# Attention scores of one layer as 64-row float32 products, and feed-forward transposes in groups of eight

## The chip, the cores and the metric

The kernel runs on one core of one Trainium2 chip. The metric is device time in microseconds of one execution. TensorE (PE) multiplies, VectorE (DVE) and ScalarE (ACT) do element-wise work and empty the accumulators, GpSimd (POOL) does small vectors, and SyncE (SP) issues all DMA transfers.

## The reference

Two decoder layers over 256 tokens of width 1024, all in float32. What matters here of a layer:

```
q, k, v, s_in, c_in, g_in = split(rms_norm(x) @ w_in)
qh, kh = partial_rope(q), partial_rope(k)        # 8 query heads, 2 key heads, head width 64
scores = qh . kh * 64 ** -0.5                    # each token sees the 128 tokens up to itself
m = max(max(scores), sink);  pr = exp(scores - m)
y_attn = (pr / (sum(pr) + exp(sink - m)) @ v) @ w_attn_out
y_ssm, y_conv = (state-space branch of s_in), (convolution branch of c_in)
x = x + (gates[0] * y_attn + gates[1] * y_ssm + gates[2] * y_conv) @ w_mix_out
f_gate, f_up = split(rms_norm(x) @ w_ffn_in)     # hidden width 2816
x = x + (silu(f_gate) * f_up) @ w_ffn_out
x = x + sigmoid(rms_norm(x) @ w_ple_gate) * (p @ w_ple_in)
```

## The kernel before

The tokens are two tiles of 128 (`t` = 0, 1) and lie on the partitions. Every large product is a `gemm` (lines 447 to 479): pairs of 128-row blocks of a weight matrix are loaded as float32 (`raw`), ScalarE rounds them to float32r (`wh`), VectorE takes the difference (`wl`), and for each token tile and block TensorE adds three products of 512 columns, high by high, high by low and low by high. Left operands are brought to the same two parts by `split` (lines 229 to 234): a ScalarE copy and a VectorE difference. Transposes (line 281) are TensorE products with a float32 identity; they go to two banks of PSUM named `tr`, accumulators to four banks named `mm`, the attention's and the state-space branch's products to two named `sm`.

The order of the work is made while the program is built. A `gemm` calls `pump` (lines 391 to 400) after each six products. The small work is written as generators (`Stream`), each with a priority; they stop at points such as `on_pe`, `on_dve`, `on_act`, and `pump` runs a stream on if the planner's clocks (`run`, lines 122 to 142, with a cost per instruction) say that what it needs is ready. Each engine then works through its own list in that fixed order. In layer 0 the order of the gemms is `zk zq zc g00 g10 g11 g21 g01 y0 g20 y1 u1 c0 c1 u0 u2 u3` (line 34): the projections, the gates `g`, the attention output `y` (tiles `ya`), the state-space output `u`, the convolution output `c` (tiles `yc`).

Attention (`attn_stream`, lines 834 to 926) runs once for each token tile. The keys are transposed (`kTp`), and for each of the two key heads `split` writes a 128-row copy `kz` in which the rows of the other head are zeroed by the factor `pick[g]`. The queries are transposed four times, two heads in 128 rows each (`qTp`, `qT`). Scores go to two banks; each starts with a product of the identity and the mask, and then

```
for x, y in ((0, 0), (0, 1), (1, 0)):
    mm(o, qT[x][:, c, :], kz[y][:, :, 0:nk], False, x == 1 and i == n // 2 - 1)
```

adds three float32r products that give two heads at once. Tile 0 has 128 keys and one round of eight heads; tile 1 has 256 keys and two rounds of four. VectorE takes the row maxima (line 877), ScalarE the exponentials (line 885), TensorE transposes them (`pT`) and multiplies them with the values in float32 (`po`, line 913). Beside it run the state-space branch (`ssm_prep`: `P`, `prep`, `PTi`, `CAr`, `CAi`, `kt`; `ssm_stream`: `Xr`, `Xi`, `yx`, `ge`, `gy`, `gtm`, `sT`) and the convolution (`conv_stream`: `cacc`, `cT`, `cn`, `yl`, `yt`, `cTh`).

The feed-forward input has eleven gemms `fz` of 48 products for each layer. `e_fz` (lines 1282 to 1302) empties one: a tanh for each token tile, two VectorE passes (`fth`), four transposes into one bank (`hT`), and a `split` into `hdh` and `hdl`. The feed-forward output `fo` reads these pairs in order, `hid[k // 2]`, from the first on (line 1312).

Of the kernel before, what the change touches and what calls it, by code (L numbers as in the profile page):

```python
# [6 lines left out]
F32 = mybir.dt.float32  # L7
F32R = mybir.dt.float32r
# [8 lines left out]
NT = 2  # L17
# [64 lines left out]
def trunk_kernel(tc, wts, par, bmat, cst_d, x_d, pos_d, pt_d, bias_d, fg_d, out_d, dbg=None):  # L82
# [3 lines left out]
    with ctx:  # L86
# [8 lines left out]
        def b2(shape, dt=F32, name="b2"):  # L95
            return act.tile(shape, dt, tag="b2", bufs=25, name=name)
# [56 lines left out]
        def p_tr(name):  # L153
            return rotate(ps.tile([128, 512], F32, tag="tr", bufs=2, name=name), "tr", 2)
# [74 lines left out]
        def split(hi, lo, src, scale=None):  # L229
            copy(hi, src, scale)  # L230
            if scale is None:
                tt(lo, src, hi.bitcast(F32), ALU.subtract)
            else:
                stt(lo, src, scale, hi.bitcast(F32), ALU.mult, ALU.subtract)
# [44 lines left out]
        def transpose(out, in_):  # L279
            run("pe", PE_TR, [out], [in_])  # L280
            PE.transpose(out, in_, ident)
# [120 lines left out]
        def on_pe(*tiles, into=None):  # L402
            if into is None:
                n = f"tr.{(turn.get('tr', -1) + 1) % 2}"
                banks = [(n, 0), (n, 1)] if TRCHK else []
            else:
                banks = [k for b in into for k in keys(b)]
            return "pe", tiles, banks
# [423 lines left out]
            tt(z2, ra[:, 2], ra[:, 3], ALU.add)  # L832

        def attn_stream(t, S):
            zqk, vt, kz, par_l = S["zqk"], S["vt"], S["kz"], S["par"]
            nk = 128 * (t + 1)
            hpt = 1024 // nk
            mk = maskr[:, 256 - nk:256]
            z = zqk[t]
            yield lambda: S["rope_ok"]  # L840
            yield on_dve(z)
            rope_step(t, z)
            yield on_pe(z)
            zf = z.rearrange("p h d -> p (h d)")
            pt = p_tr("kTp")
            transpose(pt[:, 0:128], zf[:, 512:640])
            for g in range(2):
                split(kz[0][:, g, 128 * t:128 * t + 128], kz[1][:, g, 128 * t:128 * t + 128], pt[:, 0:128], pick[g])
            S["k_done"] += 1
            pt = p_tr("qTp")  # L850
            for k in range(4):
                transpose(pt[:, k * 128:k * 128 + 128], zf[:, k * 128:k * 128 + 128])
            qT = [b2([128, 4, 128], F32R, name=f"qT{i}") for i in range(2)]
            split(*[w.rearrange("p a b -> p (a b)") for w in qT], pt, 0.125)
            yield lambda: S["k_done"] > t
            st = act.tile([128, 6, 8], F32, tag="ast", bufs=4, name="ast")
            sink = par_l[:, O_SINK:O_SINK + 8]
            scs = []
            for b in range(8 // hpt):
                sc = b4([128, hpt, nk], name="sc")  # L860
                scs.append(sc)
                yield from sm_units.take(2)
                pts = [p_sm("sc").rearrange("p (i k) -> p i k", k=nk) for _ in range(2)]
                yield on_pe(*qT, *kz, into=pts)
                n = hpt // 2
                for hf in range(2):
                    mm(pts[hf], identr, bc(mk, 1, n), True, False)
                    for i in range(n // 2):
                        c = (hpt * b + n * hf) // 2 + i
                        o = pts[hf][:, 2 * i:2 * i + 2]  # L870
                        for x, y in ((0, 0), (0, 1), (1, 0)):
                            mm(o, qT[x][:, c, :], kz[y][:, :, 0:nk], False, x == 1 and i == n // 2 - 1)
                sl = slice(hpt * b, hpt * b + hpt)
                for hf in range(2):
                    yield on_dve(pts[hf])
                    run("dve", 615, [st], [pts[hf]])
                    DVE.reduce_max(out=st[:, 0, hpt * b + n * hf:hpt * b + n * hf + n], in_=pts[hf], axis=AX.X)
                yield on_dve(st)
                tt(st[:, 1, sl], st[:, 0, sl], sink[:, sl], ALU.max)
                tt(st[:, 2, sl], sink[:, sl], st[:, 1, sl], ALU.subtract)  # L880
                ts(st[:, 1, sl], st[:, 1, sl], -1.0, ALU.mult)
                for i in range(hpt):
                    yield on_act(st)
                    slot = hpt * b + i
                    func(sc[:, i], pts[i // n][:, i % n], AF.Exp, bias=st[:, 1, slot:slot + 1],
                         accum_out=st[:, 4, slot:slot + 1])
                sm_units.give(2)
            yield on_act(st)
            func(st[:, 3, :], st[:, 2, :], AF.Exp)
            yield on_dve(st)  # L890
            tt(st[:, 4, :], st[:, 4, :], st[:, 3, :], ALU.add)
            recip(st[:, 5, :], st[:, 4, :])
            pTs = {}
            for g in range(2):
                for kb in range(t + 1):
                    yield on_pe(*scs)
                    pt = p_tr("pT")
                    for i in range(4):
                        slot = 4 * g + i
                        transpose(pt[:, i * 128:i * 128 + 128],  # L900
                                  scs[slot // hpt][:, slot % hpt, kb * 128:kb * 128 + 128])
                    pT = b2([128, 4, 128], name="pTs")
                    copy(pT.rearrange("p h q -> p (h q)"), pt)
                    pTs[g, kb] = pT
            yield from sm_units.take(1)
            po = p_sm("po")
            yield on_pe(*pTs.values(), into=[po])
            for g in range(2):
                for i in range(4):
                    slot = 4 * g + i  # L910
                    kv = slot % 2
                    for kb in range(t + 1):
                        mm(po[:, slot * 64:slot * 64 + 64], pTs[g, kb][:, i, :], vt[kb][:, kv * 64:kv * 64 + 64],
                           kb == 0, kb == t)
            o = b2([128, 8, 64], name="o")
            yield on_dve(po, st)
            tt(o, po.rearrange("p (h d) -> p h d", h=8), bc(st[:, 5, :], 2, 64), ALU.mult)
            sm_units.give(1)
            yield on_pe(o)
            of = o.rearrange("p h d -> p (h d)")  # L920
            pt = p_tr("oT")
            for k in range(4):
                transpose(pt[:, k * 128:k * 128 + 128], of[:, k * 128:k * 128 + 128])
            hi, lo = b2([128, 4, 128], F32R, name="aTh"), b2([128, 4, 128], F32R, name="aTl")
            split(hi.rearrange("p a b -> p (a b)"), lo.rearrange("p a b -> p (a b)"), pt)
            S["aT"][t] = (hi, lo)
# [164 lines left out]
        def layer(l, feat, sts, prep):  # L1091
# [4 lines left out]
            hrstd = [stat(sts, 5, t) for t in range(NT)]  # L1096
            S["zqk"] = [act.tile([128, 10, 64], F32, tag="zqk", bufs=2, name="zqk") for t in range(NT)]
            S["vt"] = [act.tile([128, 128], F32, tag="vt", bufs=2, name="vt") for t in range(NT)]
            S["kz"] = [b2([128, 2, 256], F32R, name="kz") for i in range(2)]
            S["Ux"] = Ux = b2([128, 8, 64], name="Ux")  # L1100

            def e_zk(acc):
# [179 lines left out]
            def e_fz(acc):  # L1282
                yield on_act(*acc)
                ths = []
                for t in range(NT):
                    th = b1([128, 256], name="fth")
                    func(th, acc[t][:, 0:256], AF.Tanh, scale=stat(fst, 5, t))
                    ths.append(th)
                for t in range(NT):
                    yield on_dve(ths[t])  # L1290
                    stt(ths[t], ths[t], 1.0, acc[t][:, 0:256], ALU.add, ALU.mult)
                for t in range(NT):
                    stt(ths[t], acc[t][:, 256:512], stat(fst, 6, t), ths[t], ALU.mult, ALU.mult)
                yield on_pe(*ths)
                pt = p_tr("hT")
                for t in range(NT):
                    for k in range(2):
                        o = (2 * t + k) * 128
                        transpose(pt[:, o:o + 128], ths[t][:, k * 128:k * 128 + 128])
                hi, lo = b2([128, NT, 2, 128], F32R, name="hdh"), b2([128, NT, 2, 128], F32R, name="hdl")  # L1300
                split(hi.rearrange("p t k q -> p (t k q)"), lo.rearrange("p t k q -> p (t k q)"), pt)
                hid.append((hi, lo))

            for c in range(11):
                gemm(fT[0], 8, "fz", FFNB, e_fz, fT[0].need if c == 0 else None)
            split(pTh.rearrange("p a b -> p (a b)"), pTl.rearrange("p a b -> p (a b)"),
# [345 lines left out]
```

## Time and profile before

| | |
|---|---|
| median of 3 runs | 827.81 us (827.27 to 830.09) |
| profiled execution, its own time | 828.6 us |
| its span, first to last instruction | 826.8 us |
| mean granted clock of TensorE | 0.996 of full |
| TensorE busy | 810.5 us, 98% |
| VectorE, ScalarE busy | 575.9 us (70%), 479.8 us (58%) |

[...] A float32 product that is not a transpose has two records. In the timeline and the chain a line gathers equal instructions that follow each other.

### The profile page before, as it was taken

The numbers are of one execution on the slowest core, as the hardware profiler recorded it, in microseconds if no ns is written. First come the engines' busy times: TensorE is split into PE (matmuls) and PEld (weight loads), VectorE is DVE, ScalarE is ACT, GpSimd is POOL, SyncE is SP. The second block draws the span as 40 slices with busy tenths as digits, with TensorE's granted clock in tenths as the row PEclk, the third lists the DMA queues.
The fourth block names the chain that finished last, engine by engine and source line by source line (L and its number), as shares of the span: only waits on it lengthen the run. The fifth ranks groups of instructions, "written<-read, shape, count | busy, mean of one in ns | idle before, by whom it ended". The sixth has DMA issues, their size and how long they took to land.

```text
span 826.8 us, 11001 instructions
## 1 busy us (share of the span) xinstructions
PE 810.5 (98%) x3904; PEld 672.6 (81%) x3904; DVE 575.9 (70%) x876; ACT 479.8 (58%) x783; POOL 115.7 (14%) x310
## 2 busy tenths in 40 slices
PE   8999999899999999999999999999999999999996
PEld 6787888778888888888888888878888888888885
DVE  4589998696676875554578789877766666655455
ACT  6678856665546665553664675667554445445363
POOL 6784000000837000000110000100010000000011
PEclk9999999999999999999999999999999999999999
DMA  7755536456656655666655453766666666666661
GB/s 260 235 174 148 148 113 185 133 166 203 188 174 186 179 174 164 184 179 204 178 153 161 158 158 106 232 206 202 178 194 193 185 182 179 191 188 180 202 186 68
DMA packets 43685, 146.33 MB, mean 177 GB/s; under 512 B 4976, under 2 KB 6384, under 8 KB 43632
## 3 DMA queue, kind: packets, MB, share of 16 engines
q1 hardware_dynamic: 43632, 145.65, 58.3%
q8 instruction: 30, 0.49, 0.2%
q14 instruction: 23, 0.19, 0.1%
HBM read 144.58 MB, written 1.05 MB: 176 GB/s over the span
## 4 chain that ended last, share of the span: by engine, by line
PE 85%; DVE 5%; ACT 4%; DMA 3%; issue 1%; SPq 0%; POOLq 0%; POOL 0%; ACTq 0%; DVEq 0%
PE fz L227 27%; PE g L227 15%; PE fo L227 14%; PE mo L227 5%; DMA raw<-in_wts 3%; PE ya L227 2%; PE pz L227 2%; DVE wl L200 2%; PE u L227 2%; PE zc L227 2%; ACT wh L176 2%; PE pl L227 1%; PE zq L227 1%; PE ez L227 1%; PE yx L227 1%; PE po L227 1%
## 5 line engine op out<-in xcount | busy, mean ns | idle before, releaser
L200 DVE TENSOR_TENSOR wl<-raw,wh 128x1024 fp32r<-128x1024 f32 (+1 forms) x261 | 315.9, 1213 | 196.9 <-ACT wh L176 196.8
L176 ACT CAST wh<-raw 128x1024 fp32r<-128x1024 f32 (+1 forms) x261 | 272.4, 1046 | 187.9 <-PE fo L227 57.1
L200 POOL TENSOR_TENSOR nst<-nst 128x2 f32<-128x2 f32 (+1 forms) x14 | 2.8, 200 | 494.2 <-ACT sqj L171 493.7
L227 PE MATMUL fz<-wh,f0h 128*128 128x512 f32 x176 | 70.1, 398 | 0.0
L227 PE MATMUL fz<-wh,f1h 128*128 128x512 f32 x176 | 69.6, 395 | 0.0
L227 PE MATMUL fo<-wh,hdh 128*128 128x512 f32 x176 | 68.8, 391 | 0.0
L227 PE MATMUL fz<-wh,f0l 128*128 128x512 f32 x176 | 68.7, 390 | 0.0
L227 PE MATMUL fz<-wh,f1l 128*128 128x512 f32 x176 | 68.6, 390 | 0.0
L227 PE MATMUL fz<-wl,f0h 128*128 128x512 f32 x176 | 68.6, 390 | 0.0
L227 PE MATMUL fz<-wl,f1h 128*128 128x512 f32 x176 | 68.6, 390 | 0.0
L227 PE MATMUL fo<-wh,hdl 128*128 128x512 f32 x176 | 68.5, 389 | 0.0
L227 PE MATMUL fo<-wl,hdh 128*128 128x512 f32 x176 | 68.5, 389 | 0.0
L227 PEld LDWEIGHTS fz<-wh,f0l 128*128 128x128 f32 x176 | 33.0, 188 | 7.1
L227 PEld LDWEIGHTS fz<-wh,f1l 128*128 128x128 f32 x176 | 33.0, 188 | 7.0
L227 PE MATMUL g<-wh,h1h 128*128 128x512 f32 x96 | 38.2, 398 | 0.6 <-ACT g L171 0.6
L227 PEld LDWEIGHTS fo<-wh,hdl 128*128 128x128 f32 x176 | 33.0, 188 | 6.9
L227 PEld LDWEIGHTS fo<-wl,hdh 128*128 128x128 f32 x176 | 33.0, 188 | 6.8
L227 PEld LDWEIGHTS fo<-wh,hdh 128*128 128x128 f32 x176 | 33.0, 188 | 6.7
L227 PE MATMUL g<-wh,h0h 128*128 128x512 f32 x96 | 38.5, 401 | 0.0
L227 PEld LDWEIGHTS fz<-wl,f1h 128*128 128x128 f32 x176 | 33.1, 188 | 6.5
L227 PEld LDWEIGHTS fz<-wh,f1h 128*128 128x128 f32 x176 | 33.1, 188 | 6.5
L227 PEld LDWEIGHTS fz<-wl,f0h 128*128 128x128 f32 x176 | 33.1, 188 | 6.4
(377 smaller groups left out, 1739.5 us busy)
## 6 DMA issues: line engine op xcount, KB each, us to landing
raw<-in_wts SPq DMA_DIRECT2D x258, 512.0 KB, 3.6
brow<-in_bias SPq DMA_DIRECT2D x20, 256.0 KB, 4.3
raw<-in_wts SPq DMA_DIRECT2D x4, 256.0 KB, 3.8
out<-e SPq DMA_DIRECT2D x4, 256.0 KB, 2.0
x<-in_x SPq DMA_DIRECT2D x4, 128.0 KB, 3.8
x<-in_x SPq DMA_DIRECT2D x2, 256.0 KB, 5.4
bm<-in_bmat SPq DMA_DIRECT2D x4, 128.0 KB, 6.0
pT<-in_pt SPq DMA_DIRECT2D x2, 256.0 KB, 4.4
```

Of the source, the lines that this page charges most:

```text
L176: ACT.copy(out=out, in_=in_)
L200: (eng or DVE).tensor_tensor(out=out, in0=a, in1=b, op=op)
L227: PE.matmul(out, lhsT, rhs, start=start, stop=stop, skip_group_check=onto)
```

## The change

In layer 0 the keys are kept once, in float32 (`kT`, one ScalarE copy for each tile), and so are the queries (`qT`, one scaled copy). For each head one float32 product is made from the 64 rows in which the head lies: rows 0 to 63 for the heads of the first bank, 64 to 127 for those of the second. The two banks then hold every other head, and the maxima and exponentials are addressed accordingly. Layer 1 keeps the zero-padded keys. In the feed-forward of both layers `e_fz` keeps the result of every other gemm back, and transposes two together into both banks `tr`; the eleventh is alone.

```diff
@@ attn_stream
             pt = p_tr("kTp")
             transpose(pt[:, 0:128], zf[:, 512:640])
-            for g in range(2):
+            if kT is not None:
+                copy(kT[:, 128 * t:128 * t + 128], pt[:, 0:128])
+            for g in range(2 if kT is None else 0):
                 split(kz[0][:, g, 128 * t:128 * t + 128], kz[1][:, g, 128 * t:128 * t + 128], pt[:, 0:128], pick[g])
...
-            qT = [b2([128, 4, 128], F32R, name=f"qT{i}") for i in range(2)]
-            split(*[w.rearrange("p a b -> p (a b)") for w in qT], pt, 0.125)
+            if kT is None:
+                qT = [b2([128, 4, 128], F32R, name=f"qT{i}") for i in range(2)]
+                split(*[w.rearrange("p a b -> p (a b)") for w in qT], pt, 0.125)
+            else:
+                qT = [b2([128, 4, 128], name="qT")]
+                copy(qT[0].rearrange("p a b -> p (a b)"), pt, 0.125)
...
-                yield on_pe(*qT, *kz, into=pts)
+                yield on_pe(*qT, *(kz if kT is None else [kT]), into=pts)
                 n = hpt // 2
                 for hf in range(2):
                     mm(pts[hf], identr, bc(mk, 1, n), True, False)
-                    for i in range(n // 2):
+                    rows = slice(64 * hf, 64 * hf + 64)
+                    for i in range(n if kT is not None else 0):
+                        mm(pts[hf][:, i], qT[0][rows, b * n + i, :],
+                           kT[rows, 128 - nk + 128 * t:128 * t + 128], False, i == n - 1)
+                    for i in range(n // 2 if kT is None else 0):
...
-                    DVE.reduce_max(out=st[:, 0, hpt * b + n * hf:hpt * b + n * hf + n], in_=pts[hf], axis=AX.X)
+                    mx = st[:, 0, hpt * b + n * hf:hpt * b + n * hf + n]
+                    if kT is not None:
+                        mx = st[:, 0, sl].rearrange("p (i f) -> p f i", f=2)[:, hf]
+                    DVE.reduce_max(out=mx, in_=pts[hf], axis=AX.X)
...
-                    func(sc[:, i], pts[i // n][:, i % n], AF.Exp, bias=st[:, 1, slot:slot + 1],
+                    ps_i = pts[i // n][:, i % n] if kT is None else pts[i % 2][:, i // 2]
+                    func(sc[:, i], ps_i, AF.Exp, bias=st[:, 1, slot:slot + 1],
@@ layer
-            S["kz"] = [b2([128, 2, 256], F32R, name="kz") for i in range(2)]
+            S["kT"] = act.tile([128, 256], F32, tag="kT", bufs=1, name="kT") if l == 0 else None
+            S["kz"] = [b2([128, 2, 256], F32R, name="kz") for i in range(2)] if l else None
@@ layer, e_fz
-                yield on_pe(*ths)
-                pt = p_tr("hT")
...
+                pend.append(ths)
+                fzs[0] += 1
+                if len(pend) < 2 and fzs[0] < 11:
+                    return
+                group = list(pend)
+                pend.clear()
+                banks = [(f"tr.{b}", i) for b in range(2) for i in range(2)]
+                yield "pe", [a for g in group for a in g], banks
+                pts = [p_tr("hT") for g in group]
+                for g, pt in zip(group, pts):
...
+                            transpose(pt[:, o:o + 128], g[t][:, k * 128:k * 128 + 128])
+                for pt in pts:
+                    hi, lo = b2([128, NT, 2, 128], F32R, name="hdh"), b2([128, NT, 2, 128], F32R, name="hdl")
+                    split(hi.rearrange("p t k q -> p (t k q)"), lo.rearrange("p t k q -> p (t k q)"), pt)
+                    hid.append((hi, lo))
```

The planner's costs change with the instructions, so the order of much of layer 0 moves. Three places show it.

First, TensorE at the first scores of layer 0, before: the scores of tile 0, and then the key and query transposes of tile 1, a gemm later than those of tile 0.

```order
L227 MATMUL sc<-maskr,identr 128x512
L227 MATMUL sc<-kz,qT_741 128x256 x2
L227 MATMUL sc<-kz,qT_742 128x256
L227 MATMUL sc<-kz,qT_741 128x256 x2
L227 MATMUL sc<-kz,qT_742 128x256
L227 MATMUL sc<-maskr,identr 128x512
L227 MATMUL sc<-kz,qT_741 128x256 x2
L227 MATMUL sc<-kz,qT_742 128x256
L227 MATMUL sc<-kz,qT_741 128x256 x2
L227 MATMUL sc<-kz,qT_742 128x256
L281 MATMUL kTp<-cst,zqk 128x128
L281 MATMUL qTp<-cst,zqk 128x128 x4
```

And now, the transposes of both tiles and the scores of tile 0:

```order
L281 MATMUL kTp<-cst,zqk 128x128
L281 MATMUL qTp<-cst,zqk 128x128 x4
L281 MATMUL kTp<-cst,zqk 128x128
L281 MATMUL qTp<-cst,zqk 128x128 x4
L227 MATMUL sc<-maskr,identr 128x512
L227 MATMUL sc<-kT,qT 128x128 x4
L227 MATMUL sc<-maskr,identr 128x512
L227 MATMUL sc<-kT,qT 128x128 x4
```

The five transposes of tile 1 have moved up by 24 products, to stand right behind those of tile 0.

Second, ScalarE from the copies `PTi` of the state-space preparation to the gate ahead of `ya`, before:

```order
L176 COPY PTi<-prep 128x512 x2
L171 ACTIVATE gt<-g_0_994,nst 128x512
L171 ACTIVATE gt<-g_1_995,nst 128x512
L176 CAST wh<-raw 128x1024
L176 CAST aTh<-oT 128x512
L176 COPY CAr<-v_1329 64x8x4x16 x2
L176 CAST wh<-raw 128x1024 x3
L171 ACTIVATE gt<-g_0_1131,nst 128x512
L171 ACTIVATE gt<-g_1_1132,nst 128x512
L176 COPY CAi<-v_1391 64x8x4x16 x2
```

And now (`cn`, `yl`, `yt`, `cTh` are the end of the convolution branch):

```order
L176 COPY PTi<-prep 128x512 x2
L171 ACTIVATE cn<-cT,cst 128x256 x2
L171 ACTIVATE yl<-cT_1432,cst 128x256 x2
L171 ACTIVATE yt<-yl 128x512
L176 COPY CAr<-v_1405 64x8x4x16 x2
L176 COPY CAi<-v_1444 64x8x4x16 x2
L171 ACTIVATE cTh<-yl 128x512
L176 CAST wh<-raw 128x1024
L171 ACTIVATE gt<-g_0_1165,nst 128x512
L171 ACTIVATE gt<-g_1_1166,nst 128x512
```

The convolution's end, which stood behind the attention output, now stands between `PTi` and the tanh `gt` of gate `g01`.

Third, TensorE now, at the start of `ya`; twelve products of gate `g01` (tiles `g_0_1165`, `g_1_1166`) stand between the four transposes `cT` of `cn` and these rows:

```order
L227 MATMUL ya_1494<-wh,aTh 128x512
L227 MATMUL ya_1494<-wl,aTh 128x512
L227 MATMUL ya_1494<-wh,aTl 128x512
L227 MATMUL kt<-BB,CAr 128x32
L227 MATMUL kt<-BB,CAi 128x32
L227 MATMUL kt<-BB,CAr 128x32
L227 MATMUL kt<-BB,CAi 128x32
L227 MATMUL ya_1495<-wh,aTh 128x512
```

Before, `cT` stood behind the first `ya`; the built program lets the first product into `ya_1495` wait for ScalarE's `gt` of `g_1_1166`.

## Rows read from the trace of the kernel before

**Rows 1.** The page, busy time of each engine.

```profile
PE 810.5 (98%) x3904; PEld 672.6 (81%) x3904; DVE 575.9 (70%) x876; ACT 479.8 (58%) x783; POOL 115.7 (14%) x310
```

**Rows 2.** The view of waits, TensorE: total, times, longest, in us.

```profile
PE sT L281 <- DVE gtm L214: 1.6, 1, 1.6
...
PE u L227 <- ACT sTh L171: 0.7, 1, 0.7
```

**Rows 3.** The view of windows: length, busy of each engine, granted clock, DMA share, GB/s.

```profile
105.00:120.00 15.00, 15.00 (x89) 13.11 (x88) 14.90 (x26) 7.82 (x11) 0.00 (x0) 1.00 0.30 91
158.20:161.60 3.40, 3.40 (x9) 2.64 (x9) 1.92 (x3) 0.56 (x2) 0.00 (x0) 0.50 0.34 99
```

**Rows 4.** TensorE's timeline, first scores: start us, us, what.

```profile
60.10 0.87 PE L227 MATMUL sc<-kz,qT 128*128 128x256 f32 x6
60.81 0.27 PE L281 MATMUL kTp<-cst,zqk 128*128 128x128 f32 x1
```

**Rows 5.** TensorE's timeline, first pT transposes and tile 1's first scores.

```profile
69.53 2.75 PE L281 MATMUL pT<-cst,sc 128*128 128x128 f32 x8
72.04 0.48 PE L227 MATMUL sc<-maskr,identr 128*128 128x512 f32 x1
72.35 0.85 PE L227 MATMUL sc<-kz,qT 128*128 128x512 f32 x3
73.04 0.39 PE L227 MATMUL sc<-maskr,identr 128*128 128x512 f32 x1
```

**Rows 6.** TensorE's timeline, po.

```profile
101.13 2.56 PE L227 MATMUL po<-vt,pTs 128*128 128x64 f32 x22
```

**Rows 7.** The groups by line and shape, a product and a weight load of fo.

```profile
L227 PE MATMUL fo<-wl,hdh 128*128 128x512 f32 x176 | 68.5, 389 | 0.0
...
L227 PEld LDWEIGHTS fo<-wl,hdh 128*128 128x128 f32 x176 | 33.0, 188 | 6.8
```

**Rows 8.** The chain in order of time, feed-forward of layer 1: start us, us, what.

```profile
664.08 0.44 PE hT L281 x4
...
686.81 0.44 PE hT L281 x4
```

**Rows 9.** The chain, first products of fo without transposes.

```profile
734.79 25.39 PE fo L227 x112
```

**Rows 10.** The chain, feed-forward of layer 0 from the last features on.

```profile
203.98 0.87 PE f0p L281 x8
204.86 12.28 PE fz L227 x54
```

**Rows 11.** TensorE's timeline, first transposes of the attention.

```profile
51.92 0.39 PE L227 MATMUL g<-wh,h0l 128*128 128x512 f32 x1
52.48 0.33 PE L281 MATMUL kTp<-cst,zqk 128*128 128x128 f32 x1 [0.17 <-ACT ubuf L176]
52.94 0.33 PE L281 MATMUL qTp<-cst,zqk 128*128 128x128 f32 x1
```

**Rows 12.** ScalarE's groups from 45 to 180 us: busy us, mean ns, idle before.

```profile
L176 ACT CAST wh<-raw 128x1024 fp32r<-128x1024 f32 x35 | 36.7, 1056 | 10.7 <-PE g L227 6.1 <-DMA raw<-in_wts 2.4 <-PE yc L227 1.8
L171 ACT ACTIVATE gt<-g,nst 128x512 f32<-128x512 f32 x12 | 7.9, 696 | 1.1 <-PE g L227 1.1
...
L176 ACT COPY CAr<-v 64x512 f32<-64x512 f32 x2 | 1.2, 620 | 3.0 <-DVE v L200 2.9
...
L176 ACT COPY PTi<-prep 128x512 f32<-128x512 f32 x2 | 1.1, 590 | 3.8 <-PE prep L281 3.8
...
L171 ACT ACTIVATE yl<-cT,cst 128x256 f32<-128x256 f32 x2 | 1.0, 560 | 0.7 <-PE cT L281 0.7
...
L171 ACT ACTIVATE cTh<-yl 128x512 fp32r<-128x512 f32 x1 | 0.6, 632 | 0.0
```

**Rows 13.** ScalarE's timeline, two gate tanhs in a row.

```profile
144.06 1.26 ACT L171 ACTIVATE gt<-g,nst 128x512 f32<-128x512 f32 x2
```

**Rows 14.** VectorE's groups from 45 to 180 us.

```profile
L210 DVE SCALAR_TENSOR_TENSOR qT<-qTp,qT 128x512 fp32r<-128x512 f32 x2 | 1.4, 691 | 0.3
```

More of the change, by code (lines that the diff above doesn't have):

```diff
@@ L834, in attn_stream @@
         def attn_stream(t, S):
-            zqk, vt, kz, par_l = S["zqk"], S["vt"], S["kz"], S["par"]
+            zqk, vt, kz, kT, par_l = S["zqk"], S["vt"], S["kz"], S["kT"], S["par"]
             nk = 128 * (t + 1)
@@ L1293, in e_fz @@
                     stt(ths[t], acc[t][:, 256:512], stat(fst, 6, t), ths[t], ALU.mult, ALU.mult)
-                yield on_pe(*ths)
-                pt = p_tr("hT")
[L1296 to L1302, printed above, removed]
+                pend.append(ths)
[8 more added lines that the diff above has]
+                for g, pt in zip(group, pts):
+                    for t in range(NT):
+                        for k in range(2):
+                            o = (2 * t + k) * 128
+                            transpose(pt[:, o:o + 128], g[t][:, k * 128:k * 128 + 128])
[3 more added lines that the diff above has]
+                    hid.append((hi, lo))
+            pend, fzs = [], [0]
             for c in range(11):
```

## The prediction

> **What bounds the kernel.** I read the page first: TensorE is busy for 810.5 of 826.8 us, so a microsecond counts only if it is one of TensorE's [rows 1]. The view of waits, for TensorE, comes second: its own idle time is small and sits in a few places of layer 0, the longest 1.6 us before the transposes of `sT` and 0.7 us behind them [rows 2]. The windows come third: from 105 to 120 us VectorE is 99% busy (14.90 of 15.00) while TensorE has no gap, so VectorE's load there costs nothing. From 158.2 to 161.6 us the granted clock is 0.50, so TensorE ran at 1.2 instead of 2.4 GHz; the spell follows the `sT` gaps and loses half of 3.4 us, 1.7 us [rows 3]. The timeline and the chain of TensorE give the price of each shape. So I count TensorE's time for each edit, then its waits.
>
> **Score products, layer 0.** Before, tile 0 has two groups of six products of 256 columns. The second takes 60.10 to 60.81, 0.71 us, the first about as long [rows 4]. Tile 1 has four groups of three products of 512 columns, 72.35 to 73.04, 0.69 us each [rows 5]. That is 2 x 0.71 + 4 x 0.69 = 4.2 us. The six mask products stay. Now there are 8 products of 128 columns and 8 of 256, in float32. Such a product is two records in the trace: 22 records of `po`, 64 columns each, take 2.56 us, 0.11 per record [rows 6]. What a record of 128 or 256 columns costs no row shows. From below: one streaming each, 0.11 for 128 columns and 0.1175 for 256 (0.71 / 6), 3.6 us in all, 0.6 less than before. From above: four streamings each (the 0.11 of 64 columns would allow it), 0.227 and 0.453, 10.9 us, 6.7 more. I take two streamings, since two records of two streamings make the four partial products of a high and a low half: 16 records at 0.1175 and 16 at 0.227, 5.5 us. **+1.3 us.**
>
> The products have 64 rows and stand between mask products of 128 rows, so the shape of the array in use changes four times in each of three blocks, 12 times. No row has such a change. From below it is free (a gain is excluded: a mask product over all rows stands between the two halves, so they cannot run side by side). From above it ends all overlap: a product of 512 columns lasts 0.389 us but the next starts 0.227 after it, a tail of 0.16, and a weight load of 0.188 would come behind it [rows 7], 12 x 0.35 = 4.2 us. The nearest change the trace has, from float32 transposes back to 512-column products, costs 0.04 to 0.05 (next part); half a tail, 0.08, lies between that and a full one, and I take it. **+1.0 us.** The Trainium skill, TensorEngine Tiling (Array Packing), Key Properties, says that changing the tiling mode drains TensorE; no row here shows it, and by it each change would pay the full 0.16 and the sum would be 1.0 us higher.
>
> **Feed-forward transposes.** 112 products of `fo` take 25.39 us, 0.2267 each. Two rounds of 48 products and four transposes take 664.08 to 686.81, 22.73 us; less 96 x 0.2267 = 21.76 that leaves 0.97, 0.485 per group of four. The group of eight at 203.98 and the 54 products behind it take until 217.14, 13.16 us; less 12.24 that leaves 0.92 [rows 8 to 10]. So a pair of fours becomes an eight for 0.05 less. Each layer has eleven groups, now five pairs and a single: 10 x 0.05. **-0.5 us**, between nothing and -1.0 (10 x 0.1, were the cost of going back to products all there is). Nothing is released late by it: the hidden features are read only after the last `fz` product but for the last group, which stays alone and stands inside `fo` as before. The evacuations then come in twos, on engines that have idle time there.
>
> **Waits in layer 0.** The planner now moves the attention stream. Gone: eight `pT` transposes stood where each waited for its own exponential on ScalarE, 69.53 to 72.04, 2.51 us where eight take 0.87 [rows 5]. In the new order 36 gate products stand between tile 0's scores and `pT`. **-1.6 us.**
>
> New at the first scores: tile 1's `kTp` and `qTp` follow tile 0's at once (shown in the section on the change). The bank for `kTp` is one that ScalarE must empty first. Before, tile 0's two transposes already wait there, 52.48 - 51.92 - 0.23 = 0.33 us and 52.94 - 52.48 - 0.11 = 0.35 [rows 11], behind ScalarE's `ubuf` copies. Tile 1's now wait for the copies of tile 0's, which stand behind a `wh` cast of 1.06 us [rows 12]: about 0.7 and 0.4. **+1.1 us**, from nothing (ScalarE ahead) to 1.5.
>
> New at `prep`: the last eight transposes come four and four; the other bank holds `cT` until `cn`, which ScalarE now does behind both `PTi` copies (shown there too). So the second four wait out a tail, a copy of 0.59 [rows 12] and the hand-offs. **+0.8 us.**
>
> New at `ya`: the first product into its second bank waits for the tanh `gt` of the gate ahead. ScalarE does that now behind two `yl`, `yt`, four `CAr`/`CAi`, `cTh`, a `wh` cast and the first `gt`, and all of this begins only when TensorE has done `cT`. With [rows 12] that is 2 x 0.56 + 0.63 + 4 x 0.62 + 0.63 + 1.06 + 2 x 0.70 = 7.3 us, less 0.1 for each of ten overlaps (two `gt` in a row take 1.26, not 1.39 [rows 13]), 6.3, with hand-offs 6.4. TensorE in that time has 12 gate products, 6 of `ya` and 8 records of `kt`: 18 x 0.227 + 8 x 0.11 = 5.0 us. **+1.4 us**, from nothing to 2.
>
> Not counted: VectorE loses the differences of `kz` and `qT`, two of 0.69 [rows 14] and four shorter ones, under 3 us in all, in a stretch where TensorE does not wait for it. The `sT` gap I leave as it is: it is a chain from `yx` on TensorE through `ge` and `gy`, not VectorE's backlog. Layer 1 keeps its products, so nothing there.
>
> **Sum.** 1.3 + 1.0 - 0.5 - 1.6 + 1.1 + 0.8 + 1.4 = +3.5 us. The profiled execution took 828.6 us (span 826.8), 0.8 above the median of 827.81. 828.6 + 3.5 = 832.1, less 0.8 gives **831.3** as a median. A measurement of this kernel tells about 0.3% from no change, 2.5 us: below 825.3 is faster, above 830.3 slower.
>
> **Rivals.**
> - *No change.* The changes of shape are free and half of the new waits (3.3 us) are covered because ScalarE runs ahead of where I put it: 3.5 - 1.0 - 1.6 = +0.9, 828.7. For it: every wait is worked out to some tenths, from queues that hold ten instructions. Against: the `ya` wait is a loop from TensorE through ScalarE and back, which does not shift with either engine. 24%.
> - *Faster, by the state-space chain.* If the time freed on VectorE brings `gtm` forward by 1.6 us or more, the `sT` wait of 1.6 goes, the 0.7 behind it, and the half-clock spell of 1.7 us: -4.0. With the changes of shape free and the `ya` wait hidden, 3.5 - 4.0 - 1.0 - 1.4 = -2.9, 824.9. It decides only from 1.6 us on. Against: `gtm` follows `yx`, and `yx` stands after the same products. 14%.
> - *Drained and reloaded at each change of shape.* 12 x 0.35 instead of 12 x 0.08: 3.2 more, 834.5. For it: nothing in the trace overlaps across such a change. 12%.
> - *Four streamings per record.* 10.9 instead of 5.5 us: 5.4 more, 836.7. The `po` rows don't exclude it. 5%.
> - *The forecast*, 829 to 834: 45%.
>
> **How the numbers follow.** Slower: 45 + 12 + 5, less 5 for the forecast's lower edge, 57%. Same: 24 + 5 = 29%. Faster: 14%. The range leaves out most of the faster case and the four streamings: 827 to 836.
>
> **What would show it.** The `kT` products: 16 records 0.12 apart and 16 some 0.23 apart; 0.11 or 0.45 would be the bounds. The gap between a mask product and the first 64-row product shows the price of the change of shape. `hT` in groups of eight, 0.92 each. `pT` some 0.11 apart at its first place. TensorE idle about 0.7 before tile 1's `kTp`, 0.8 inside `prep`, 1.4 before the second `ya` bank, with ScalarE's `gt` as releaser. The `sT` wait still near 1.6 and one spell of half clock. I am wrong if the waits at `ya` and `prep` are missing, if the spell is gone, or if a second one appears.

## The result, and the profile after

The changed kernel takes 835.08 us (median of 5 runs, 832.8 to 836.39), the kernel before 827.81 beside it (5 runs, 827.27 to 830.09): ratio 1.0075, 95% interval 1.006 to 1.009. It is slower, as forecast, and inside the range, but by 7.3 us where 3.5 were forecast. The profiled execution took 832.8 us, span 830.7: 4.2 and 3.9 more than the profiled execution before. So the sum nearly holds between the two traces, and the rest lies between the runs. Their mean granted clocks go with their times; 0.004 of 830 us is 3.3 us, and the first and the last run lie 3.6 apart:

| run of the change, us | 832.8 (profiled) | 834.46 | 835.08 | 835.72 | 836.39 |
|---|---|---|---|---|---|
| mean granted clock | 0.995 | 0.993 | 0.993 | 0.991 | 0.991 |

A spell of 3.4 us at half clock takes 0.002 off the mean. The mean also counts the end of the span, where the clock falls behind TensorE's last product: in the trace of `both_fill` (below) it stands at 0.50 from 825.9 us to the end at 829.4, with no spell before, and the mean is 0.998. In the kept traces 0.997 to 0.999 goes with no spell, and 0.995 or 0.996 with one.

The page of the change; TensorE is still the bound [rows 1]:

```profile
PE 813.1 (98%) x3912; PEld 676.0 (81%) x3912; DVE 573.5 (69%) x870; ACT 479.6 (58%) x781; POOL 123.2 (15%) x310
```

The view of waits of the change, for TensorE:

```profile
PE ya L227 <- ACT gt L171: 1.9, 1, 1.9
PE sT L281 <- DVE gtm L214: 1.3, 1, 1.3
...
PE prep L281 <- ACT PTi L176: 0.7, 1, 0.7
```

The two forecast waits are there, `ya` on ScalarE's `gt` and `prep` on `PTi`; the one before `sT` is 1.3 instead of 1.6 [rows 2]. TensorE's timeline of the change, at the first scores (start us, us, what, idle before):

```profile
52.86 0.33 PE L281 MATMUL kTp<-cst,zqk 128*128 128x128 f32 x1 [0.17 <-ACT ubuf L176]
...
54.34 0.33 PE L281 MATMUL kTp<-cst,zqk 128*128 128x128 f32 x1 [0.36 <-ACT kT L176]
54.84 0.66 PE L281 MATMUL qTp<-cst,zqk 128*128 128x128 f32 x4 [0.17 <-ACT qT L171]
55.25 0.48 PE L227 MATMUL sc<-maskr,identr 128*128 128x512 f32 x1
55.66 1.16 PE L227 MATMUL sc<-kT,qT 64*128 64x128 f32 x8
56.74 0.51 PE L227 MATMUL sc<-maskr,identr 128*128 128x512 f32 x1
...
58.26 0.50 PE L227 MATMUL g<-wh,h0h 128*128 128x512 f32 x1
58.60 0.39 PE L227 MATMUL g<-wl,h0h 128*128 128x512 f32 x1
...
66.55 1.03 PE L281 MATMUL pT<-cst,sc 128*128 128x128 f32 x8
67.34 0.48 PE L227 MATMUL sc<-maskr,identr 128*128 128x512 f32 x1
67.75 1.13 PE L227 MATMUL sc<-kT,qT 64*128 64x256 f32 x4
68.81 0.51 PE L227 MATMUL sc<-maskr,identr 128*128 128x512 f32 x1
...
70.30 0.50 PE L227 MATMUL g<-wh,h0h 128*128 128x512 f32 x1
...
77.24 0.39 PE L227 MATMUL sc<-maskr,identr 128*128 128x512 f32 x1
...
80.11 0.50 PE L227 MATMUL g<-wh,h0h 128*128 128x512 f32 x1
```

Records of products overlap (a product of 512 columns is 0.39 long, and the next starts 0.23 after it), so costs are read from start to start. The kernel before, at the same places:

```profile
58.92 0.39 PE L227 MATMUL sc<-maskr,identr 128*128 128x512 f32 x1
...
73.96 0.39 PE L227 MATMUL g<-wh,h0h 128*128 128x512 f32 x1
...
84.88 0.39 PE L227 MATMUL sc<-maskr,identr 128*128 128x512 f32 x1
...
86.73 1.03 PE L281 MATMUL prep<-cst,P 128*128 128x128 f32 x8
...
100.90 0.39 PE L227 MATMUL g<-wh,h0l 128*128 128x512 f32 x1
```

A block of scores now takes 58.26 - 55.25 = 3.01 us for tile 0 and 70.30 - 67.34 = 2.96 and 80.11 - 77.24 = 2.87 for the halves of tile 1, and the product behind it is followed after 0.34 instead of 0.23: 3.01 + 2.96 + 2.87 + 3 x 0.11 = 9.2 us. Before, it was 60.81 - 58.92 = 1.89 [rows 4], 73.96 - 72.04 = 1.92 [rows 5] and 86.73 - 84.88 = 1.85, 5.7 in all. The products alone are what was forecast: in the single records the starts lie 0.112 apart at 128 columns and 0.216 at 256, two streamings, 16 x 0.112 + 16 x 0.216 = 5.2 us. From a mask product to the first 64-row record it is 0.32 instead of 0.23 behind gate products (77.24), 0.41 behind transposes and 0.44 behind 64-row products. That first record is followed after 0.21 instead of 0.11, or after 0.32 instead of 0.22 at 256 columns. A block of tile 0 without changes of shape would take 2 x (0.227 + 8 x 0.112) = 2.25, one of tile 1 2 x (0.227 + 4 x 0.216) = 2.18. So the four changes cost 2.87 + 0.11 - 2.18 = 0.80 in the last block. In the other two it is 3.01 + 0.11 - 2.25 = 0.87 and 2.96 + 0.11 - 2.18 = 0.89, with 0.08 in each for the transposes ahead, behind which a mask product took 0.31 before as well (72.04 to 72.35 [rows 5]). That is **0.2 us each, 2.4 for the twelve.** It is not the change from float32r to float32 that costs on the way in: in the kernel before the float32 products `po`, of 128 rows, start 0.23 behind a gate product (100.90 to 101.13) and then 0.11 apart, with nothing added [rows 6]. `pT` takes 67.34 - 66.55 = 0.79 where the eight took 2.51 [rows 5].

ScalarE's timeline of the change, ahead of the `ya` wait, and TensorE's around it:

```profile
124.21 1.02 ACT L171 ACTIVATE yl<-cT,cst 128x256 f32<-128x256 f32 x2 [3.85 <-PE cT L281]
...
125.80 1.23 ACT L176 COPY CAr<-v 64x512 f32<-64x512 f32 x2
...
128.33 0.63 ACT L171 ACTIVATE cTh<-yl 128x512 fp32r<-128x512 f32 x1
...
129.80 1.26 ACT L171 ACTIVATE gt<-g,nst 128x512 f32<-128x512 f32 x2
...
128.82 0.39 PE L227 MATMUL kt<-BB,CAi 128*128 128x32 f32 x2
131.11 0.50 PE L227 MATMUL ya<-wh,aTh 128*128 128x512 f32 x1 [1.90 <-ACT gt L171]
```

It is the forecast queue in the forecast order, from 124.21 to 131.06: 6.85 us where 6.3 were worked out. TensorE waits for its end: the view of waits has 1.9 us, and from start to start it is 131.11 - 128.94 - 0.11 = 2.06, where 128.94 is the start of the second `kt` record. Behind this wait further half-clock spells begin in other runs (below). The view of windows of the change:

```profile
128.90:131.20 2.30, 0.40 (x4) 0.29 (x3) 2.30 (x3) 2.30 (x5) 0.00 (x0) 1.00 0.00 0
131.20:150.00 18.80, 18.80 (x100) 16.08 (x101) 13.32 (x20) 12.54 (x27) 0.00 (x0) 1.00 0.51 154
...
163.86:167.27 3.41, 3.41 (x9) 2.63 (x8) 1.50 (x2) 0.38 (x1) 0.00 (x0) 0.50 0.44 119
```

In this execution the `ya` wait (128.90 to 131.20) is followed by full clock, and the one spell of 3.4 us stands behind the `sT` wait, as before [rows 3]. It is the fastest of the five runs.

The chain of the change, feed-forward of layer 1:

```profile
656.59 0.87 PE hT L281 x8
657.47 21.78 PE fz L227 x96
679.25 0.87 PE hT L281 x8
```

A round of eight transposes and 96 products takes 679.25 - 656.59 = 22.66, less 21.76 is 0.90; two groups of four took 0.97 [rows 8]. That is 0.07 for each pair.

### The profile page after: what moved, and what is told of

It is laid out like the page before. It is cut to its first block, busy times and chain, and to the rows that moved or that the text cites. A ratio compares the mean times of both kernels' runs of the same rounds, so it can differ in the third digit from the quotient of the medians.

```text
span 830.7 us, 11003 instructions
## 1 busy us (share of the span) xinstructions
PE 813.1 (98%) x3912; PEld 676.0 (81%) x3912; DVE 573.5 (69%) x870; ACT 479.6 (58%) x781; POOL 123.2 (15%) x310
## 4 chain that ended last, share of the span: by engine, by line
PE 88%; ACT 4%; DVE 4%; DMA 2%; issue 1%; SPq 0%; POOLq 0%; POOL 0%; ACTq 0%; DVEq 0%
PE fz L227 29%; PE g L227 14%; PE fo L227 14%; PE mo L227 5%; PE pz L227 4%; DMA raw<-in_wts 2%; PE ya L227 2%; DVE wl L200 2%; PE u L227 2%; PE zc L227 2%; PE sc L227 1%; PE pl L227 1%; PE zq L227 1%; PE ez L227 1%; PE zk L227 1%; PE yx L227 1%
```

## The experiments

### One part of the change alone

`g8_only` is the kernel before with the `e_fz` part of the diff alone; `attn_only` has the attention part alone.

> The kernel before with the feed-forward transposes in groups of eight and nothing else. Theory (the loss is all in the attention of layer 0): 0.5 to 1 us less than before, about 827.0, with no new wait of TensorE. Rival (the part of the loss that the profiled run of the change does not show comes from the larger groups, which hold both transpose banks at once): slower than before by 2 us or more, with waits at hT.

> The changed attention of layer 0 with the transposes in groups of four as before. Theory: 0.5 to 1 us more than the whole change, about 835.8, with the same waits before kTp (0.4), inside prep (0.7) and at ya (1.9). Rival (the groups of eight carry half of the loss): about 831.

Measured: `g8_only` 826.7 us (11 runs, 824.89 to 827.46), ratio 0.9981 (0.9972 to 0.999); `attn_only` 837.15 (6 runs, 834.19 to 840.41), ratio 1.0111 (1.009 to 1.0131); the kernel before beside them 828.06. The groups of eight save 1.4 us, and no wait at `hT` came, so that rival is out. The attention part costs 9.1; its 837.15 lies above the 835.8 expected. The runs of `g8_only` fall in two lots: five of 824.89 to 825.6 at clocks of 0.997 to 0.999, six of 826.7 to 827.46, all at 0.995. The lots lie 1.7 us apart, what one spell of 3.4 us loses. Its profiled run, 824.89, has the `sT` wait of 1.6 and full clock behind it, as its view of windows shows:

```profile
150.00:175.00 25.00, 21.69 (x96) 16.57 (x95) 22.68 (x40) 16.92 (x28) 0.00 (x0) 1.00 0.44 141
```

The runs of `attn_only` go from 834.19 at 0.997 to 840.41 at 0.988. The view of windows of its profiled run, 840.41:

```profile
132.70:146.30 13.60, 13.60 (x46) 11.67 (x45) 9.46 (x16) 3.07 (x5) 0.00 (x0) 0.50 0.40 133
```

Right behind the `ya` wait, TensorE runs 13.6 us at 1.2 GHz without one gap, and it loses half of that. That is what the expectation of 835.8 left out. So the spells, and not the sum alone, had to be tested.

### The changes of shape

`masks_first` writes both mask products ahead, then all products of rows 0 to 63, then those of 64 to 127; a block has two changes instead of four. `alternate` has the same with the halves in turn (the two loops exchanged).

```diff
-                    rows = slice(64 * hf, 64 * hf + 64)
-                    for i in range(n if kT is not None else 0):
-                        mm(pts[hf][:, i], qT[0][rows, b * n + i, :], ...
+                    if kT is not None and hf == 1:
+                        for h2, i in [(h, j) for h in range(2) for j in range(n)]:
+                            rows = slice(64 * h2, 64 * h2 + 64)
+                            mm(pts[h2][:, i], qT[0][rows, b * n + i, :], ...
```

> The whole change, but in each block of scores both mask products come first, then the 64-row products of rows 0 to 63, then those of rows 64 to 127. The array's shape then changes twice in a block and not four times; the rows in use change once without a change of shape. Theory (a change of shape costs 0.2 us): 6 fewer of them, 1.2 us less than the change, and 0.1 to 0.2 us between the first and the second half at most. Rival (the 0.2 is paid whenever the rows change, drained or not): 3 fewer, 0.6 less.

> As the run with both masks first, but the 64-row products alternate between rows 0 to 63 and rows 64 to 127. Theory (products on different rows of the array run side by side): the 32 records of the products take down to half of their 5.2 us, so up to 2.6 us less than with both masks first, 3.8 less than the change. Rival (each change of rows drains, 0.1 to 0.2 us): 13 more such changes, 1.3 to 2.6 us more than with both masks first.

Measured: `masks_first` 831.61 us (6 runs, 829.85 to 833.73), ratio 1.0046 (1.0031 to 1.006); `alternate` 831.42 (6 runs, 829.77 to 833.58), ratio 1.0042 (1.0026 to 1.0058). TensorE's timeline of `masks_first`:

```profile
55.07 0.71 PE L227 MATMUL sc<-maskr,identr 128*128 128x512 f32 x2
55.71 1.71 PE L227 MATMUL sc<-kT,qT 64*128 64x128 f32 x16
57.35 0.50 PE L227 MATMUL g<-wh,h0h 128*128 128x512 f32 x1
...
66.44 0.71 PE L227 MATMUL sc<-maskr,identr 128*128 128x512 f32 x2
67.09 1.14 PE L227 MATMUL sc<-kT,qT 64*128 64x256 f32 x8
68.16 0.50 PE L227 MATMUL g<-wh,h0h 128*128 128x512 f32 x1
```

And of `alternate`:

```profile
55.95 0.71 PE L227 MATMUL sc<-maskr,identr 128*128 128x512 f32 x2
56.59 1.16 PE L227 MATMUL sc<-kT,qT 64*128 64x128 f32 x16
57.68 0.50 PE L227 MATMUL g<-wh,h0h 128*128 128x512 f32 x1
```

The blocks of `masks_first` take 2.28, 1.72 and 1.63 us, 3.2 less than the change's 8.8, which is most of the 3.5 in the medians. Two changes less in each block would give 6 x 0.2 = 1.2, the whole of what was expected. The rest is something else: the products of the two halves run side by side. In tile 1 eight records take 1.07 (67.09 to 68.16) where four took 1.06 in the change. In `alternate` 16 records take 1.09 (56.59 to 57.68), where eight took 1.08. So the position of the rows may change for nothing; the shape, 64 rows after 128, costs 0.2. The Trainium skill, TensorEngine Tiling (Array Packing), Key Properties, says both: another tiling mode drains TensorE, and different tiles work independently. This case's rows agree in that the change of shape costs and the change of rows does not. With the halves side by side the three blocks of `alternate` take 1.73, 1.71 and 1.78, and 3 x 0.11 behind them, 5.5 us, where the zero-padded products took 5.7. `alternate` saves 0.55 more than `masks_first` in tile 0, and yet its median is only 0.2 lower. Apart from the score products, every engine works through its list in the same order in both, but in the profiled run of `alternate` TensorE waits longer elsewhere. The view of waits of `alternate`, for TensorE:

```profile
PE po L227 <- ACT sc L171: 0.9, 1, 0.9
PE prep L281 <- ACT PTi L176: 0.9, 1, 0.9
PE zc L227 <- ACT zqk L171: 0.9, 1, 0.9
```

In the view of `masks_first` the one before `po` is missing, and the others are 0.8 and 0.6. The one before `zc` stands ahead of the scores, so it is not from this edit; why ScalarE's `sc` comes later here is open. Both keep the `ya` wait of 1.9 and the `sT` wait of 1.3, and both show clocks down to 0.991 and 0.990.

### The wait before `ya`, removed

`cT_later` is the change, with the second part of the convolution held until the first attention output `y0` and half of the gate gemm `g20` behind it are done, so that `yl`, `yt` and `cTh` no longer stand ahead of `gt`.

```diff
@@ conv_stream
+            if S["kT"] is not None:
+                yield lambda: flow["mm"] >= 36
             yield on_pe(cn)
```

> The whole change, but in layer 0 the convolution branch may go on to its second transposes (cT of cn) only after the first attention-output gemm and half a gate gemm, so that yl, yt and cTh no longer stand ahead of gt on ScalarE. Theory (the gap at ya costs its 1.9 us, and in most runs one or more half-clock spells of 1.7 us lost each behind it): the wait at ya gone or under 1 us, 1.5 to 2 us less by the gap, and the granted clock of the runs back to 0.995 to 0.998; about 831 as a median. Rival (the spells have nothing to do with this gap): 1.9 us less at most, with the clock of the runs still 0.991 to 0.995.

Measured: 828.38 us (11 runs, 827.55 to 829.76), ratio 1.0009 (0.9999 to 1.0018), clocks 0.996 to 0.998 in every run. That is 6.7 us below the change by one generator's stop, and 2.6 below what was expected. Its profile has no wait at `ya`, and none before `sT` either, since the transposes there now find `gtm` done: 1.9 + 1.3 = 3.2 us. A new one stands a few products behind, in its view of waits:

```profile
PE u L227 <- DVE sTl L210: 0.7, 1, 0.7
```

So 2.5 us of waiting are gone. Its view of windows, over the place of the former `ya` wait:

```profile
120.00:134.00 14.00, 14.00 (x95) 12.70 (x95) 12.19 (x20) 8.22 (x12) 0.00 (x0) 1.00 0.16 55
```

The remaining 4.2 of the 6.7 have no wait to go with them. The stop moves other work too, so that this run alone does not show what they are; the filled waits below give 4.0 for the spells.

### The waits kept, and filled

`g8_fill` is `g8_only` with 12 thrown-away products added right before `sT`. `ya_fill` is the change with 14 of them before the first product into the second `ya` bank, and `both_fill` has 9 before `sT` as well. All three do this work beside the reference's; the waits for `gt` and `gtm` stay as they are, and in `ya_fill` and `both_fill` no other instruction moves. `after_again` is the change itself, in the same job as the last two.

```diff
@@ gemm, ahead of the first product into acc[1] of the first ya
+                        for _ in range(14):
+                            PE.matmul(pt[:, 0:256], identr, maskr, start=True, stop=True)
@@ ssm_stream, behind pt = p_tr("sT")
+                for _ in range(9):
+                    PE.matmul(pt[:, 0:256], identr, maskr, start=True, stop=True)
```

> The kernel before with groups of eight, and twelve products of the mask with the identity (256 columns, 0.117 us each, 1.4 us in all) put right before the sT transposes of layer 0, into the bank that these overwrite. They do work that is thrown away, in a gap in which TensorE waits 1.6 us. Theory (half-clock spells follow the idle time there): the filling is free, no run has a spell behind it, clock 0.997 to 0.999 in all runs, and the median goes to the lower of the two levels that the runs with groups of eight alone show, 825.3. Rival (the spell does not depend on idle time): the clock as without the filling, 0.995 in about half of the runs, and the same median, 826.7.

> The change, with 14 thrown-away products of 256 columns (mask by identity, into a transpose bank) added on TensorE right before the first product into ya's second bank, where it has waited 1.9 us for gt. Nothing else moves. Theory (the idle wait brings further spells of half clock, and these are the 3 us by which the median of the change lies above the sum of its terms): the products fill the wait and add nothing to it, no run is below a clock of 0.995 and the median falls from 835.1 to 832 to 833.3, since the one spell behind the sT gap stays. Rival (the spells come of themselves, or from elsewhere): median 835 or more, clocks down to 0.991 as before. Second rival: the products are on the path, 1.6 us more, 836.7.

> The same, and 9 thrown-away products right before the transposes sT of layer 0, where TensorE waits 1.3 us for gtm. Theory: no spell of half clock behind either gap; the median falls by 3 to 4.7 us against the change, to 830.4 to 832, with clocks of 0.997 and more in nearly all runs, though no wait has become shorter. That would be the price of the edits and waits at full clock. Rival: 835 or more.

> The change as it is, beside the two with filled waits, on the same chip: 833 to 836.5, with clocks of 0.991 to 0.995. Lower, at 0.997, would mean that the chip and not the wait sets the number of spells.

Measured:

| kernel | median, us | runs | ratio to before | granted clocks |
|---|---|---|---|---|
| `g8_fill` | 825.62 (824.85 to 826.49) | 10 | 0.9973 (0.9964 to 0.9983) | 0.997 (9 runs), 0.999 |
| `after_again` | 835.07 (831.05 to 839.04) | 6 | 1.0077 (1.0058 to 1.0096) | 0.987, 0.993 (4 runs), 0.998 |
| `ya_fill` | 832.06 (831.47 to 832.38) | 5 | 1.005 (1.0038 to 1.0063) | 0.995 to 0.997 |
| `both_fill` | 831.02 (830.26 to 831.25) | 5 | 1.0037 (1.0025 to 1.005) | 0.997 to 0.998 |

`g8_fill` has no run at 0.995, where `g8_only` had six of eleven; its 12 products take 1.7 us in the place of the 1.6 us wait, so that the lower lot of times stays about where it was and the upper one is gone. The two ran on different chips, with the kernel before at 827.61 beside `g8_fill` and at 828.06 beside `g8_only`; for the change, `after_again`, `ya_fill` and `both_fill` ran on one chip. TensorE's timeline of `ya_fill`: the filling ends when `gt` comes, and `ya` starts at 131.27 where it was 131.11 in the change, in a run that is 0.16 later before it too.

```profile
129.20 1.91 PE L471 MATMUL fill<-maskr,identr 128*128 128x256 f32 x14
131.27 0.50 PE L227 MATMUL ya<-wh,aTh 128*128 128x512 f32 x1 [0.16 <-ACT gt L171]
```

More work makes the kernel 3.0 us faster with one wait filled and 4.0 with both, and the spread falls from 8 us to 1. The view of windows of `after_again`, its slowest run:

```profile
131.00:135.00 4.00, 3.87 (x16) 3.45 (x17) 4.00 (x8) 3.18 (x5) 0.00 (x0) 0.69 0.40 131
135.00:148.00 13.00, 13.00 (x44) 10.92 (x43) 6.88 (x10) 1.91 (x3) 0.00 (x0) 0.57 0.41 135
```

And of `both_fill`, the same stretches and the one behind `sT`:

```profile
131.00:135.00 4.00, 3.85 (x21) 3.26 (x21) 4.00 (x8) 3.31 (x5) 0.00 (x0) 1.00 0.42 131
135.00:148.00 13.00, 13.00 (x67) 10.97 (x66) 8.05 (x12) 7.41 (x20) 0.00 (x0) 1.00 0.55 183
...
163.00:168.00 5.00, 5.00 (x21) 3.84 (x22) 3.58 (x7) 2.58 (x4) 0.00 (x0) 1.00 0.54 184
```

From 135 to 148 us TensorE is busy throughout in both, with 44 records in the one and 67 in the other. The idle wait lowers the clock of the products behind it, but not by the same time in each run. Five kept traces have the `ya` wait unfilled: in two of them (`attn_only`, `after_again`) the clock is 0.50 for 13.7 us behind it, in one (`masks_first`) for 3.4, and in two (the change, `alternate`) not at all; no other trace has a spell there. All six traces with the `sT` wait of 1.3 us unfilled have 3.4 us at 0.50 behind it. `after_again` has one run below and one above the clocks that were expected of it. The one run of `after_again` at a clock of 0.998 took 831.05 us, as `both_fill` does. So 831.0 is what the change takes without spells, and the other 4 us of its median are spells.

### A version that beats both

`combined` is the change with `alternate`, the hold of `cT_later` and one table entry of the planner (`MIXL`, 6500 for 5500 in layer 0).

> The whole change with alternating 64-row products, with cT held back as in the run cT_later, and with the planner letting more small work in behind the products of layer 0 (its allowance 6500 instead of 5500), which moves the last prep transposes ahead of the waits. Theory (products side by side give back 0.8 us against the zero-padded ones and no change of shape but two in a block; the waits at prep, ya and sT are gone, the one before tile 1's kTp stays): 1.5 to 2.5 us less than before in the profile, no spell behind sT, about 824.5. Rival (the order makes new waits as long as those removed): 826 or more, not better than groups of eight alone.

Measured: 824.54 us (5 runs, 823.16 to 825.01), ratio 0.9957 (0.9944 to 0.997), clocks 0.997 and 0.998. The view of windows, over the stretch of the former `sT` wait:

```profile
150.00:172.00 22.00, 20.09 (x87) 15.47 (x85) 19.17 (x32) 14.00 (x23) 0.00 (x0) 1.00 0.61 199
```

Neither of the two waits nor a spell is left; the view of waits has 0.5 before `u` for `sTl`, 0.6 inside `prep` and 0.6 before a gate product instead. `combined` is 1.1 us below `g8_fill`, which has the groups of eight alone, no spell either, and ran on the same chip. So the attention part need not be a loss. How much of this each of the three edits gives was not measured, and the planner's entry was not tried on the kernel before.

## Why the prediction was right, and where its size was off

| term | forecast, us | measured, us |
|---|---|---|
| score products | +1.3 | +1.0 (5.2 instead of 5.5) |
| twelve changes of shape | +1.0 | +2.4 |
| groups of eight | -0.5 | -0.9 in layer 0, -0.4 in layer 1 |
| `pT` | -1.6 | -1.7 |
| `kTp`, `qTp` of tile 1 | +1.1 | +0.9 (0.52 and 0.39) |
| `prep` | +0.8 | +0.8 |
| `ya` | +1.4 | +2.1 |
| `sT` wait | 0 | -0.3 |
| sum | +3.5 | +3.9 |
| elsewhere | 0 | 0.0 (0.4 more ahead of the first `kTp`, 0.2 more in the rest of layer 0, 0.5 less at the start of layer 1, 0.1 less at the end), so the span's +3.9 |
| spells, run against run | none new | +3 in the median |

- **Score products.** Two streamings per record, as chosen; the rivals with one or four are out.
- **Changes of shape.** The mis-sized term. "Half a tail, 0.08" should have been 0.2, a full tail and a little more: even a full tail of 0.16 at each change, 1.9 us in all, is less than the 2.4 measured. The rival of a drain with a weight load behind it (0.35) was too dear. The bound from below excluded a gain rightly for this order of the products; `masks_first` shows that a gain was there for another.
- **Groups of eight.** Layer 1 gives five pairs at 0.07. In layer 0 0.5 more went because a group of before came late: its transposes started 0.54 behind the last product (262.19 to 262.73) instead of 0.23, and the next product 0.59 behind them instead of 0.44.
- **Waits.** They stand in the table from start to start; the view of waits, which counts from the end of the record before, has 0.7 for `prep` and 1.9 for `ya`. `kTp`, `qTp` and `prep` came as worked out from the queues. The `ya` loop was 0.7 too short, 0.5 of it since ScalarE's eleven instructions took 6.85 us: the overlaps were counted at 0.1 each and only some have it.
- **The spells.** This step failed: "one spell of half clock", taken as it was in the one trace of before. The prediction named a second spell as a sign that it would be wrong, and gave it no price. The `ya` wait was found and priced at its own length alone; its price is that length and, in most runs, products at 1.2 GHz for 3.4 us or more behind it, which lose half of that time. `ya_fill` shows it: with the wait filled and as long as before, the median falls by 3.0.
- **Faster, by the state-space chain.** It did not come: the `sT` wait fell from 1.6 to 1.3. But what the rival said of a vanished `sT` wait, that the spell goes with it, is what `cT_later` and `combined` show, with a wait of 0.7 and 0.5 for `sTl` in its place.

The forecast of the median thus came 3.8 us too low in two parts. In the profiled execution it is 0.7 (4.2 against 3.5), where the terms are off by 0.4: the changes of shape (1.4) and the `ya` wait (0.7) were too small, and the groups of eight (0.8) and four other terms (0.9) made up for most of it. The other 3.1 are the spells: the profiled run of the change lies 2.3 below its median, where that of before lay 0.8 above.

## What to carry to other kernels

Where one engine is the bound, price a new idle wait on it with what the clock does behind it, by looking at the granted clock behind the waits that the trace already has, and in several runs; harmless work in the wait is a cheap test of it. Products over part of the rows came out even here, 5.5 us against 5.7, once both parts stood next to each other, in two accumulator banks, and ran side by side; each part by itself between full-height products, they took 9.2. When a planner moves work, follow what it puts ahead of the instruction that frees an accumulator: here a stop in another stream was worth 6.7 us, where the groups of eight gave 1.4.

## What was not expected of the hardware

- 64-row float32 products on rows 0 to 63 and 64 to 127 run side by side: 16 records in 1.09 us, where eight took 1.08.
- A change between 128-row and 64-row products costs 0.2 us, part before the first product and part on it.
- After an idle wait of 1.9 us, TensorE ran at half clock for 13.7 us while it had no gap; in another trace of the same program there was no spell behind this wait, and in one of `masks_first` it lasted 3.4 us. What decides between these is open.
- Thrown-away products in two idle waits made the kernel 4 us faster (835.07 to 831.02).
